# Differential attention's scores as three 64-row products per map instead of two 128-row ones

## The chip, the core and the metric

One core of a Trainium2 chip runs the whole program in one launch. The metric is the time on the device in microseconds; the kernel before takes 2785.16 us (median of three runs, 2784.28 to 2789.13).

## What is computed

Two encoder layers over 1024 tokens of width 1024. Layer 0 mixes tokens by neighbourhood attention, layer 1 by differential attention; each is followed by a gated convolutional feed-forward part and a gated embedding. The change concerns layer 1's mixer. It has 8 heads with two maps each, of width 64:

```python
s = jnp.einsum('bhmqd,bhmkd->bhmqk', qb, k).astype(jnp.float32) + bias[None, :, None]
a = jax.nn.softmax(s, axis=-1)
w = a[:, :, 0] - lam_full * a[:, :, 1]
return jnp.einsum('bhqk,bhkd->bhqd', w.astype(v.dtype), v)
```

For each head and each map m (0 or 1), scores of 1024 queries by 1024 keys come from products over 64 elements; a bias is added; the two softmaxes are subtracted with a weight lam and multiplied with the values.

## The kernel before

**Precision.** The kernel splits a float32 operand a into a high part (a rounded to float32r, a type whose products are one TensorE instruction each in this trace, where plain float32 ones are two) and a low part (a minus the high part), and forms a product as high x high + high x low + low x high: three matmuls, `mm3` (L104 to L109). `split` (L81) makes the parts: ScalarE writes the high part (L85), VectorE the low one (L86).

**Layer 1's mixer** (`da`, L578) works through 64 chunks; a chunk is one head h = n // 8 and one tile of 128 queries. What runs in a chunk, on TensorE strictly in the order of the program, since that engine alone is scheduled by hand (the other engines' lists are ordered by the framework's scheduler):

- `da_values` (L546) of the chunk before: 16 matmuls of 128 columns (two instructions for each of 8 plain float32 products, L553) into a bank of the pool `tr`.
- `da_scores` of the next chunk, map 0, then `da_turn(n, 0)`: four transposes (L539) of the finished weights E of this chunk into a bank of `tr`, copied to SBUF by ScalarE (L542).
- `tick(0.25)`, then `da_scores` of the next chunk, map 1, then `da_turn(n, 1)`: four more transposes, copied by VectorE (L544). In the text T0 and T1 are the transposes of the two turns.
- `tick(0.25)`, `da_out` of the chunk before (one transpose, L567, into the bank that `da_values` took), `tick(0.5)`.

`tick` moves a second stream of work forward, `qkv_stream` (L228), which projects the next heads' keys, queries and values: six steps per chunk, one step being one `mm3` with 512 columns (L107 to L109). So TensorE always has projections between the attention's own pieces.

**PSUM.** Pool `s` has two buffers of two banks (scores of 128 queries by 1024 keys), `pj` two banks for projections, `tr` two banks for transposes, values and outputs. A bank is given out again once its last reader is done; the values' bank is held from the first value matmul until `da_out` behind T1.

**Queries and keys.** A projected block has map 0 of a head on partitions 0 to 63 and map 1 on 64 to 127. So that a score matmul can use all 128 rows, the evacuation puts the parts on top of each other: for map m, `Q[m]` holds the high part on the map's own half and the low part on the other one, `KH[m]` holds the keys' high part on both halves and `KL[m]` the low part on both. With these, `Q[m]` by `KH[m]` and `Q[m]` by `KL[m]` (L515, L516) give all four products of parts in two matmuls. It costs, per block of 512 tokens and per map, ScalarE's high part (64 x 512, L249 and L267), VectorE's low part (L250, L268) and for keys two copies to the other half (on GpSimd in layer 0, L252 and L253; on VectorE in layer 1, L255 and L256). A head takes two pages A and B of pool `r2`, which has four.

**Softmax** (`softmax_pre`, L360): VectorE adds the bias to the scores and finds the row's extreme (L364), ScalarE exponentiates and sums (L368). With both maps done, VectorE forms the coefficient from the two sums (L525 to L527) and the difference of the two maps in place, E (L528).

Of the kernel before, what the change touches and what calls it, by code (L numbers as in the profile page):

```python
# [8 lines left out]
F32 = mybir.dt.float32  # L9
# [29 lines left out]
class Trunk:  # L39
# [188 lines left out]
    def qkv_stream(self, layer, hT, x, first, mid):  # L228
# [7 lines left out]
        for j in range(KT):  # L236
            A = self.page(self.r2, "r2", (P, 4, SEQ), F32R)
            B = self.page(self.r2, "r2", (P, 4, SEQ), F32R)
            Q, KH, KL = [A[:, 0], A[:, 1]], [A[:, 2], A[:, 3]], [B[:, 0], B[:, 1]]
            def keys(tb):  # L240
                s = slice(tb * 512, tb * 512 + 512)
                ps, a = begun.pop(0) if begun else (self.bank(self.pj), 0)
                for kt, _ in enumerate(self.proj(wk, hT, ps, tb, a)):
                    if tb == 0 and kt == (1, 6)[layer]:
                        values()
                    yield
                for m in range(2):
                    o, far = own[m], own[1 - m]
                    nc.scalar.activation(KH[m][o, s], ps[o], AF.Copy)  # L249
                    nc.vector.tensor_tensor(out=KL[m][o, s], in0=ps[o], in1=KH[m][o, s].bitcast(F32), op=ALU.subtract)  # L250
                    if layer == 0:
                        nc.gpsimd.tensor_copy(KH[m][far, s], KH[m][o, s].bitcast(F32))  # L252
                        nc.gpsimd.tensor_copy(KL[m][far, s], KL[m][o, s].bitcast(F32))  # L253
                    else:
                        nc.vector.tensor_copy(KH[m][far, s], KH[m][o, s].bitcast(F32))  # L255
                        nc.vector.tensor_copy(KL[m][far, s], KL[m][o, s].bitcast(F32))  # L256

            def queries(tb):
                s = slice(tb * 512, tb * 512 + 512)
                ps, a = begun.pop(0) if begun else (self.bank(self.pj), 0)  # L260
                for kt, _ in enumerate(self.proj(wq, hT, ps, tb, a)):
                    if j == 0 and tb == 0:
                        mid(kt)
                    yield
                for m in range(2):
                    o, far = own[m], own[1 - m]
                    nc.scalar.activation(Q[m][o, s], ps[o], AF.Copy, scale=-0.125)  # L267
                    nc.vector.scalar_tensor_tensor(  # L268
                        out=Q[m][far, s], in0=ps[o], scalar=-0.125, in1=Q[m][o, s].bitcast(F32),
                        op0=ALU.mult, op1=ALU.subtract,  # L270
                    )
# [12 lines left out]
            self.qk[j] = Q, KH, KL  # L284
# [218 lines left out]
    def da_scores(self, x, n, m):  # L503
        nc = self.nc
        mm = nc.tensor.matmul
        h, t = n // NT, n % NT
        Q, KH, KL = self.qk[h]
        if t == 0 and m == 0:
            self.T = self.page(x, "T", (P, TW))
            nc.sync.dma_start(self.T, self.skewed[h][:, P - 1 : P - 1 + TW])  # L510
        s = self.ps.tile([P, 1024], F32, tag="s", name=self.uid("s"))
        q = Q[m][:, t * P : t * P + P]
        for half in range(2):
            w = slice(half * 512, half * 512 + 512)
            mm(s[:, w], q, KH[m][:, w], start=True, stop=False)  # L515
            mm(s[:, w], q, KL[m][:, w], start=False, stop=True)  # L516
# [11 lines left out]
        nc.vector.scalar_tensor_tensor(out=w, in0=e, scalar=c, in1=w, op0=ALU.mult, op1=ALU.add)  # L528
# [49 lines left out]
    def da(self, hT, oT, first, mid):  # L578

        N = NT * D_HEADS  # L580
        with self.tc.tile_pool(name="xa1", bufs=2, reuse_waits="tile") as x, \
# [5 lines left out]
            self.da_scores(x, 0, 0)  # L587
            self.da_scores(x, 0, 1)
            self.tick(6 / 6)
            for n in range(N + 1):  # L590
# [9 lines left out]
                if n + 1 < N:  # L600
                    self.da_scores(x, n + 1, 1)
# [624 lines left out]
```

## Time and profile before

| what | value |
|---|---|
| runs | 2784.28, 2785.16, 2789.13 us |
| profiled execution's own time | 2788.92 us |
| its span | 2787.1 us |
| mean granted clock of TensorE | 0.987 |
| layer 1's attention, by first and last score work | about 1364 to 1946 us of the span |
| score matmuls of layer 1 (L515, L516) | 256 + 256, 512 columns each |
| value matmuls (L553) and transposes (L539) | 1024 and 512, 128 columns each |

The span is the time from the first to the last instruction that the profiler saw. A busy share counts time with at least one instruction in work; matmuls overlap their neighbours, so the distance between two starts, and not a duration, says how long one keeps TensorE. The profile lists TensorE's weight loads (PEld) apart from its matmuls (PE). A form such as `128*128 128x512` gives rows and columns of the array in use, then the operand's partitions and columns.

### The profile page before, as it was taken

The page shows a single profiled execution, that of the slowest core. Times are in us where ns is not written, and L with a number is a line of the kernel's source. Part 1 is how long each engine was busy: PE and PEld are TensorE (multiplying, and loading weights), DVE is VectorE, ACT ScalarE, POOL GpSimd, SP SyncE. Part 2 cuts the span into 40 slices and gives each one's busy share as a digit, 9 for nine tenths or more (in the row PEclk, how much of TensorE's full clock was granted, in tenths as well). Part 3 has the DMA queues.
Part 4 walks back from the last instruction along what each step waited for, and adds up shares of the span by engine and source line. Part 5 has one row for each costly group of instructions (what it writes and reads, how often), then busy time and mean ns, then how long its engine had stood idle before and what let it go on. Part 6 is the DMA issues. An engine that isn't in the chain of part 4 may idle for free.

```text
span 2787.1 us, 36499 instructions
## 1 busy us (share of the span) xinstructions
PE 2706.9 (97%) x13312; PEld 2260.9 (81%) x13312; DVE 1983.3 (71%) x3393; ACT 1341.0 (48%) x2477; POOL 495.0 (18%) x473
## 2 busy tenths in 40 slices
PE   7999999989999999999999999999989999999999
PEld 5788887868888888878888888887868888888877
DVE  5677776678777777666677777786687776777664
ACT  4555556444444435454455555566444444444442
POOL 2121220024433400001000000000023343300000
PEclk9999999999999999999999999999989999999999
DMA  6412214623332283343211111115413333372442
GB/s 187 164 52 67 64 49 157 156 81 106 106 110 91 106 283 107 102 147 106 98 45 45 45 45 45 38 43 177 136 68 106 108 105 106 112 270 92 118 141 99
DMA packets 129188, 298.48 MB, mean 107 GB/s; under 512 B 11720, under 2 KB 37704, under 8 KB 129008
## 3 DMA queue, kind: packets, MB, share of 16 engines
q1 hardware_dynamic: 129008, 296.15, 32.4%
q8 instruction: 104, 1.70, 0.3%
q14 instruction: 76, 0.62, 0.1%
HBM read 221.69 MB, written 86.61 MB: 111 GB/s over the span
## 4 chain that ended last, share of the span: by engine, by line
PE 89%; DMA 5%; DVE 3%; ACT 2%; issue 1%; SPq 0%; POOL 0%; ACTq 0%; DVEq 0%; POOLq 0%
PE b L107 21%; PE b L109 20%; PE b L108 20%; PE g L637 6%; PE m L637 5%; PE b L553 4%; PE s L515 2%; PE s L516 2%; PE b L539 2%; PE b L135 2%; PE av L426 2%; DVE r L86 1%; PE b L410 1%; DMA x<-in_x 1%; DMA raw<-in_qkv 1%; DMA raw<-in_ple_w_gate 1%
## 5 line engine op out<-in xcount | busy, mean ns | idle before, releaser
L107 PE MATMUL b<-r,ws 128*128 128x512 f32 (+1 forms) x1312 | 541.0, 412 | 3.2 <-ACT ws L85 3.2
L109 PE MATMUL b<-r,ws 128*128 128x512 f32 (+1 forms) x1312 | 512.9, 391 | 0.5 <-DVE ws L86 0.5
L108 PE MATMUL b<-r,ws 128*128 128x512 f32 (+1 forms) x1312 | 512.1, 390 | 0.6 <-DVE r L86 0.5
L107 PE MATMUL b<-r,wa 128*128 128x512 f32 x704 | 276.5, 393 | 28.1 <-ACT wa L85 27.2
L368 ACT ACTIVATE E<-E,mn 128x1024 f32<-128x1024 f32 (+2 forms) x256 | 221.6, 866 | 148.4 <-DVE mn L364 146.6
L109 PEld LDWEIGHTS b<-r,ws 128*128 128x128 f32 x1312 | 248.3, 189 | 53.3 <-DVE ws L86 1.0
L119 POOL TENSOR_TENSOR ss<-ss,mhalf 128x1 f32<-128x1 f32 x136 | 87.5, 644 | 1141.0 <-DVE ss L557 566.0
L107 PEld LDWEIGHTS b<-r,ws 128*128 128x128 f32 x1312 | 249.6, 190 | 48.8 <-ACT ws L85 3.6
L108 PEld LDWEIGHTS b<-r,ws 128*128 128x128 f32 x1312 | 250.0, 191 | 37.6 <-DVE r L86 1.9
L108 PE MATMUL b<-r,wa 128*128 128x512 f32 x704 | 275.8, 392 | 0.0
L109 PE MATMUL b<-r,wa 128*128 128x512 f32 x704 | 275.6, 391 | 0.0
L107 PE MATMUL b<-r,r 128*128 128x512 f32 x680 | 269.3, 396 | 5.0 <-DVE v L899 2.8
L108 PE MATMUL b<-r,r 128*128 128x512 f32 x680 | 265.4, 390 | 0.0
L109 PE MATMUL b<-r,r 128*128 128x512 f32 x680 | 265.3, 390 | 0.0
L86 DVE TENSOR_TENSOR r<-raw,r 128x512 fp32r<-128x512 f32 (+1 forms) x178 | 140.8, 795 | 111.8 <-ACT r L85 111.5
L85 ACT ACTIVATE r<-raw 128x512 fp32r<-128x512 f32 (+1 forms) x178 | 121.4, 687 | 205.2 <-PE b L108 166.2
L86 DVE TENSOR_TENSOR ws<-raw,ws 128x512 fp32r<-128x512 f32 (+3 forms) x168 | 155.3, 932 | 65.3 <-ACT ws L85 63.8
L85 ACT ACTIVATE ws<-raw 128x512 fp32r<-128x512 f32 (+3 forms) x168 | 124.3, 748 | 143.3 <-PE b L109 57.0
L637 PE MATMUL g<-r,ws 128*128 128x512 f32 x768 | 182.8, 398 | 8.5 <-DVE facc L1008 8.5
L364 DVE CUSTOM_DVE_ANT_0 E<-s,T 128x1024 f32<-128x1024 f32 x128 | 156.5, 1224 | 33.5 <-PE s L516 32.5
L107 PEld LDWEIGHTS b<-r,wa 128*128 128x128 f32 x704 | 133.3, 189 | 56.5 <-ACT wa L85 27.7
L637 PEld LDWEIGHTS g<-r,ws 128*128 128x128 f32 x768 | 146.4, 192 | 39.6 <-DVE facc L1008 9.4
(178 smaller groups left out, 5332.3 us busy)
## 6 DMA issues: line engine op xcount, KB each, us to landing
raw<-in_w_in SPq DMA_DIRECT2D x88, 512.0 KB, 3.5
raw<-in_qkv SPq DMA_DIRECT2D x48, 512.0 KB, 5.7
spillS<-r SPq DMA_DIRECT2D x88, 256.0 KB, 2.5
r<-in_ffn_w_out SPq DMA_DIRECT2D x40, 512.0 KB, 10.3
raw<-spillS SPq DMA_DIRECT2D x40, 512.0 KB, 3.5
spillA<-cv SPq DMA_DIRECT2D x66, 256.0 KB, 2.6
raw<-spillA SPq DMA_DIRECT2D x30, 512.0 KB, 3.8
x<-x SPq DMA_DIRECT2D x24, 512.0 KB, 3.7
```

The costliest lines, as they stand in the source:

```text
L85: nc.scalar.activation(hi, src, AF.Copy)
L86: nc.vector.tensor_tensor(out=lo, in0=src, in1=hi.bitcast(F32), op=ALU.subtract)
L107: mm(out, sta[0], mov[0], start=first, stop=False, skip_group_check=onto)
L108: mm(out, sta[0], mov[1], start=False, stop=False, skip_group_check=onto)
L109: mm(out, sta[1], mov[0], start=False, stop=last, skip_group_check=onto)
L119: self.nc.gpsimd.tensor_tensor(out=ss, in0=ss, in1=self.mhalf, op=ALU.pow)
L135: self.nc.tensor.transpose(t[:, k * P : k * P + P], h[:, c : c + P], self.ident)
L364: nc.vector.tensor_tensor_reduce(out=e, in0=s, in1=bias, scale=1.0, scalar=3e38, op0=ALU.add, op1=ALU.min, accum_out=mn)
L368: nc.scalar.activation(e, e, AF.Exp, bias=mn, scale=-1.0, accum_out=sm)
L426: nc.tensor.matmul(out, V[:, kb, m], a[:, at * P : (at + w) * P], start=i + z == 0, stop=i == len(steps) - 1 and z == 1)
L553: nc.tensor.matmul(o, wT[:, k], V[:, k], start=k == 0, stop=k == KT - 1)
L637: mm(out[half], a, b[:, w], start=first and k + z == 0, stop=last and k == n - 1 and z == 2)
```

## The change

In layer 1, queries and keys stay where the projection puts them: one page A per head holds queries' high and low parts and keys' high and low parts (A[:, 0] to A[:, 3]), each with map 0 on partitions 0 to 63 and map 1 on 64 to 127. `split` writes each with one ScalarE and one VectorE instruction over all 128 partitions; there are no copies to the other half. `da_scores` no longer takes m: it takes both score buffers and issues, for each half of the keys, three products for each map with 64 rows, map 0 and map 1 in turn. It drops the product of the two low parts. Both softmaxes follow, and both maps' scores now lie ahead of `da_turn(n, 0)`; nothing lies between the two turns but `tick(0.25)`. Layer 0 is as before.

```diff
         for j in range(KT):
             A = self.page(self.r2, "r2", (P, 4, SEQ), F32R)
-            B = self.page(self.r2, "r2", (P, 4, SEQ), F32R)
-            Q, KH, KL = [A[:, 0], A[:, 1]], [A[:, 2], A[:, 3]], [B[:, 0], B[:, 1]]
+            if layer == 0:
+                B = self.page(self.r2, "r2", (P, 4, SEQ), F32R)
+                Q, KH, KL = [A[:, 0], A[:, 1]], [A[:, 2], A[:, 3]], [B[:, 0], B[:, 1]]
...
+                if layer == 1:
+                    self.split(ps, A[:, 2, s], A[:, 3, s])
+                    return
                 for m in range(2):
                     o, far = own[m], own[1 - m]
                     nc.scalar.activation(KH[m][o, s], ps[o], AF.Copy)
                     nc.vector.tensor_tensor(out=KL[m][o, s], in0=ps[o], in1=KH[m][o, s].bitcast(F32), op=ALU.subtract)
-                    if layer == 0:
-                        nc.gpsimd.tensor_copy(KH[m][far, s], KH[m][o, s].bitcast(F32))
-                        nc.gpsimd.tensor_copy(KL[m][far, s], KL[m][o, s].bitcast(F32))
-                    else:
-                        nc.vector.tensor_copy(KH[m][far, s], KH[m][o, s].bitcast(F32))
-                        nc.vector.tensor_copy(KL[m][far, s], KL[m][o, s].bitcast(F32))
+                    nc.gpsimd.tensor_copy(KH[m][far, s], KH[m][o, s].bitcast(F32))
+                    nc.gpsimd.tensor_copy(KL[m][far, s], KL[m][o, s].bitcast(F32))
...
+                if layer == 1:
+                    self.split(ps, A[:, 0, s], A[:, 1, s], -0.125)
+                    return
...
-            self.qk[j] = Q, KH, KL
+            self.qk[j] = (Q, KH, KL) if layer == 0 else A
...
-    def da_scores(self, x, n, m):
+    def da_scores(self, x, n):
...
-        s = self.ps.tile([P, 1024], F32, tag="s", name=self.uid("s"))
-        q = Q[m][:, t * P : t * P + P]
+        s = [self.ps.tile([P, 1024], F32, tag="s", name=self.uid("s")) for _ in range(2)]
+        q = slice(t * P, t * P + P)
         for half in range(2):
             w = slice(half * 512, half * 512 + 512)
-            mm(s[:, w], q, KH[m][:, w], start=True, stop=False)
-            mm(s[:, w], q, KL[m][:, w], start=False, stop=True)
-        e = self.page(x, f"E{m}")
+            for z, (a, b) in enumerate(((0, 2), (0, 3), (1, 2))):
+                for m in range(2):
+                    o = slice(64 * m, 64 * m + 64)
+                    nc.tensor.matmul(s[m][:, w], A[o, a, q], A[o, b, w], start=z == 0, stop=z == 2)
         a = (NT - 1 - t) * P
-        sm = self.softmax_pre(s, self.T[:, a : a + SEQ], e)
-        if m == 0:
-            self.chunk[n] = e, sm
-            return
-        w, r0 = self.chunk[n]
+        e = [self.page(x, f"E{m}") for m in range(2)]
+        r0, sm = [self.softmax_pre(s[m], self.T[:, a : a + SEQ], e[m]) for m in range(2)]
+        w = e[0]
+        self.chunk[n] = w, r0
...
-            self.da_scores(x, 0, 0)
-            self.da_scores(x, 0, 1)
+            self.da_scores(x, 0)
...
-                    self.da_scores(x, n + 1, 0)
+                    self.da_scores(x, n + 1)
                 if n < N:
                     self.da_turn(x, n, 0)
                 self.tick(0.25)
-                if n + 1 < N:
-                    self.da_scores(x, n + 1, 1)
                 if n < N:
                     self.da_turn(x, n, 1)
```

More of the change, by code (lines that the diff above doesn't have):

```diff
@@ L527, in da_scores @@
         nc.vector.reciprocal(r0, r0)
-        nc.vector.scalar_tensor_tensor(out=w, in0=e, scalar=c, in1=w, op0=ALU.mult, op1=ALU.add)
+        nc.vector.scalar_tensor_tensor(out=w, in0=e[1], scalar=c, in1=w, op0=ALU.mult, op1=ALU.add)
     def da_turn(self, x, n, g):
```

5 lines of the change are left out of this document (2 added, 3 removed).

## The prediction

> **What bounds the kernel now.** I read the page's busy shares and its chain of waits first, then the table of stretches, then the groups by shape, and last the order of time inside one chunk of layer 1's attention.
>
> ```profile
> span 2787.1 us, 36499 instructions
> ...
> PE 2706.9 (97%) x13312; PEld 2260.9 (81%) x13312; DVE 1983.3 (71%) x3393; ACT 1341.0 (48%) x2477; POOL 495.0 (18%) x473
> ...
> PE 89%; DMA 5%; DVE 3%; ACT 2%; issue 1%; SPq 0%; POOL 0%; ACTq 0%; DVEq 0%; POOLq 0%
> ```
>
> TensorE is busy for 97% of the span and carries 89% of the chain. That average must hold in the stage that changes, which runs from 1364 to 1946 us. Two stretches of it, and one near its end (columns: us, then each engine's busy time and instructions, granted clock, DMA share, GB/s):
>
> ```profile
> 1420.00:1500.00 80.00, 79.94 (x468) 68.38 (x467) 62.02 (x122) 44.77 (x91) 5.10 (x9) 1.00 0.12 40
> ...
> 1740.00:1820.00 80.00, 79.93 (x467) 68.11 (x465) 62.46 (x124) 44.44 (x89) 5.02 (x9) 1.00 0.10 34
> ...
> 1880.00:1910.00 30.00, 29.32 (x174) 24.74 (x173) 23.14 (x40) 22.29 (x42) 1.64 (x3) 1.00 0.62 213
> ```
>
> TensorE has no hole (79.9 of 80 us) at full clock, VectorE is busy for 62 and ScalarE for 44. So only TensorE's own list counts here, and what the other engines lose or gain is worth something only where TensorE comes to wait for them. Only the last few chunks have small holes, beside the loads of the output weights.
>
> One chunk (of 64) in order of time:
>
> ```profile
> 1603.15 1.95 PE L553 MATMUL b<-v,wT 128*128 128x128 f32 x16
> ...
> 1604.68 1.27 DVE L528 SCALAR_TENSOR_TENSOR E<-E,c,E 128x1024 f32<-128x1024 f32 x1
> ...
> 1604.85 0.47 PE L515 MATMUL s<-r 128*128 128x512 f32 x1
> ...
> 1605.17 0.39 PE L516 MATMUL s<-r,r 128*128 128x512 f32 x1
> ...
> 1605.40 0.40 PE L515 MATMUL s<-r 128*128 128x512 f32 x1
> ...
> 1605.63 0.40 PE L516 MATMUL s<-r,r 128*128 128x512 f32 x1
> ...
> 1606.10 0.63 PE L539 MATMUL b<-ident,E 128*128 128x128 f32 x4
> ...
> 1606.48 0.47 PE L107 MATMUL b<-r,ws 128*128 128x512 f32 x1
> ...
> 1606.76 0.60 ACT L542 ACTIVATE wT<-b 128x512 f32<-128x512 f32 x1 [1.11 <-PE b L539]
> 1606.79 0.39 PE L108 MATMUL b<-r,ws 128*128 128x512 f32 x1
> ...
> 1607.02 0.39 PE L109 MATMUL b<-r,ws 128*128 128x512 f32 x1
> ...
> 1607.25 0.40 PE L515 MATMUL s<-r 128*128 128x512 f32 x1
> ...
> 1608.17 0.60 PE L539 MATMUL b<-ident,E 128*128 128x128 f32 x4
> ```
>
> Durations of neighbours overlap, so the price of a matmul is the distance of starts: a 512-column one holds TensorE for 0.23 us (1605.17, 1605.40, 1605.63), and I use 0.231. Sixteen 128-column ones take 1604.85 - 1603.15 = 1.70 us, 0.106 each, though 128 columns at the same rate would be 0.058: there the loading of weights sets the pace, at about 0.107 us a load. The order is: sixteen value matmuls, four score matmuls of map 0, four transposes T0 (L539), one stream step of three (L107 to L109), four score matmuls of map 1, four transposes T1, then more stream steps.
>
> **The change part by part.** I take one chunk at a time and multiply by 64.
>
> **(a) The products.** Eight 128-row matmuls (8 x 0.231 = 1.848 us) become twelve 64-row ones with the same 512 columns.
>
> ```profile
> L515 PE MATMUL s<-r 128*128 128x512 f32 x256 | 106.1, 414 | 0.0
> L516 PE MATMUL s<-r,r 128*128 128x512 f32 x256 | 100.5, 392 | 0.0
> ```
>
> These are 512 in all, 8 per chunk. The trace of before has no two matmuls on different rows side by side, so the price has two ends. Lower end: the halves of a pair run in the time of one, 6 x 0.231 = 1.386 us, a gain of 0.462; the twelve weight loads, 12 x 0.107 = 1.28 us, still fit beneath. Upper end: one after another, 12 x 0.231 = 2.772, a loss of 0.924. I take the lower end: two matmuls of a pair share no rows, no operands and no PSUM bank, and the only limit of the whole engine that a row shows beside the columns, the weight load, is below it. The second half may trail the first by one load (0 to 0.107 us, once per chunk at the end of the twelve); I take 0.05.
>
> The Trainium skill, "TensorE: Matmul & The Clock Gate", Part 3, says the same of matmuls in distinct row groups (starts some 4 ns apart); no run so far shows it. By that rule the trailing would be next to nothing and the sum 3 us lower.
>
> **(b) Going from whole rows to half rows and back.** Each chunk now goes over twice: behind the values, and ahead of T0. The nearest row is layer 0's table, the only matmuls with fewer rows (32*8), first TensorE and then its weight loads:
>
> ```profile
> 55.26 0.39 PE L109 MATMUL b<-r,ws 128*128 128x512 f32 x1
> 55.58 1.88 PE L491 MATMUL b<-r,t 32*8 32x512 f32 x4
> ```
> ```profile
> 55.04 0.19 PEld L109 LDWEIGHTS b<-r,ws 128*128 128x128 f32 x1
> 55.58 0.09 PEld L491 LDWEIGHTS b<-r,t 32*8 32x8 f32 x2 [0.35 <-issue]
> ```
>
> L109 has streamed its columns by 55.26 + 0.23 = 55.49, and the first load of the other shape starts only at 55.58, for no wait that the profile shows. So a change of shape may cost 0.09 us of emptying plus a load of 0.107 that is no longer hidden: 0.20 us, twice per chunk, less the 0.05 by which the load behind the values is bare already (0.107 - 0.058): 0.35 at most. Least: nothing, if that gap belongs to the table's plain float32 and not to its rows; a gain is excluded, since nothing is removed. I take 0.20, nearer to the row, which has the same kind of step but two differences.
>
> The Trainium skill, "TensorEngine Tiling (Array Packing)", Key Properties, speaks against this change: going from one tiling mode to another drains TensorE. The 0.09 us above agrees with it; by that rule the full 0.35 stands and the sum is 10 us higher, which is the second rival.
>
> **(c) The score products no longer lie between T0 and T1.** Both maps now come ahead of T0. The pool of transposes has two banks and one holds the values' product from its first matmul to L567 behind T1, so T0 and T1 share the other: T1 must wait for ScalarE's copy L542. That copy ends at 1606.76 + 0.60 = 1607.36, 1.26 us behind T0's start. Today 0.93 us of scores cover it (T1 at 1608.17). Without them T1 would come at 1607.25, where L515 stands: a wait of 0.11, and some 0.05 to hand over: 0.16 us per chunk. Behind T1 on TensorE stand stream steps and everything else, in order, so it is paid in full. Least nothing (a bank free by another way); most 0.75, if one half-row evacuation of 0.59 us (L249 below) stands ahead on ScalarE. I take 0.16, since ScalarE was idle ahead of the copy here (1.11).
>
> **(d) T0 gets more lead.** In the chunk shown T0 starts 0.47 us behind the last score matmul and not 0.23: it waited for E, ready at 1604.68 + 1.27 = 1605.95. With map 1's scores moved up, E(n) is done some 2 us sooner. All such waits together:
>
> ```profile
> PEld b L539 <- PE s L516: 3.3, 7, 0.5
> ...
> PEld b L539 <- ACT wT L542: 0.9, 2, 0.8
> ```
>
> The L516 named had long ended, so these are E's: I take 3 us in all as won. The second row shows that the copy of (c) does hold back transposes.
>
> **(e) Splitting queries and keys.**
>
> ```profile
> L268 DVE SCALAR_TENSOR_TENSOR r<-b,r 64x512 fp32r<-64x512 f32 x64 | 44.1, 689 | 5.7 <-ACT r L267 4.0
> L250 DVE TENSOR_TENSOR r<-b,r 64x512 fp32r<-64x512 f32 x64 | 44.0, 687 | 16.0 <-ACT r L249 14.9
> L249 ACT ACTIVATE r<-b 64x512 fp32r<-64x512 f32 x64 | 37.7, 589 | 18.3 <-PE b L109 11.7 <-DVE r L250 5.2
> L86 DVE TENSOR_TENSOR r<-b,r 128x512 fp32r<-128x512 f32 x48 | 32.3, 688 | 5.4 <-ACT r L85 4.9
> L256 DVE CAST r<-r 64x512 fp32r<-64x512 f32 x32 | 13.5, 422 | 0.9
> L255 DVE CAST r<-r 64x512 fp32r<-64x512 f32 x32 | 13.5, 422 | 1.0
> ```
>
> Half of L249, L250 and L268 is layer 1's. VectorE drops 32 of 0.687, 32 of 0.689 and 64 copies of 0.422, and gains 32 of 0.688 (L86's row at full height): 71 - 22 = 49 us less; ScalarE drops about 18. All of it lies beside the 79.9 of 80 us of TensorE: nothing. If that cover were gone, up to 49 us would show, but no wait in the stretches above says so. The single page per head leaves two more pages of the pool free, so the embedding's loads and splits near the end can start sooner; TensorE did not wait for them, and I give that nothing either. Four weight loads and matmuls more per chunk are in (a).
>
> **The sum.** Per chunk -0.462 + 0.05 + 0.20 + 0.16 = -0.052 us; by 64 it is -3.3, with (d) -6.3 us. The profiled execution took 2788.9 us (span 2787.1 and 1.8 around it), so 2782.6 of its own; it lies 3.8 above the median of the runs, 2785.2, from which the same sum gives 2779.
>
> **The rivals.**
>
> *The halves run one after another.* One mechanism: TensorE gives each 64-row matmul its own 0.231 us. For it: every row of the trace shows one 512-column matmul at a time, at the same pace. Against: none has disjoint rows. Price: +0.924 + 0.20 + 0.16 = 1.28 us per chunk, +82, with (d) 79: 2864 (2841 with neither switch nor wait). It decides from a pair time of about 0.24 us upward, where the gain of (a) no longer pays for (b) and (c).
>
> *They overlap, but the switches eat it.* Full 0.35, full trailing 0.107 and 0.16: +0.155 per chunk, +10, with (d) +7: 2792; to 2815 if ScalarE is late for the copy in some chunks. For it: the gap at 55.49. Against: its different data type.
>
> *They overlap only in part.* If each half's load waits until that half's own matmul has streamed, a pair takes 0.231 + 0.107 = 0.338: 2.03 for six, +0.18 + 0.20 + 0.16 = 0.54, +35, with (d) +31: 2816. Against it stand today's loads, which start with the matmul ahead of them and not at its end:
>
> ```profile
> 1600.27 0.39 PE L107 MATMUL b<-r,ws 128*128 128x512 f32 x1
> 1600.27 0.19 PEld L108 LDWEIGHTS b<-r,ws 128*128 128x128 f32 x1
> ```
>
> *They overlap and nothing eats it.* No switch and no trailing: -0.462 + 0.16 = -0.302, -19, with (d) -22: 2763; without the T1 wait 2753.
>
> **How the numbers follow.** Forecast (2769 to 2790, likeliest 2779) 0.42; one after another 0.20; switches eat it 0.14; in part 0.08; nothing eats it 0.16. A difference of 0.2%, 5.6 us, is about what a measurement here can tell from no change, so "same" is 2779.6 to 2790.8. Of the forecast's 0.42 about 0.22 lies below that and 0.20 inside; with 0.16 that makes faster 0.38. Of the second rival 0.03 lies inside: same 0.23. The rest, 0.11 + 0.08 + 0.20, is slower: 0.39. The range leaves out the lowest part of the last rival and the upper half of the first: 2762 to 2862. The forecast's own range is 2769 to 2790.
>
> **What would show it.** In the changed profile: the two matmuls of a pair starting well under 0.23 us apart and pairs 0.23 to 0.25 apart (a); a gap ahead of the first 64-row weight load and behind the last (b); T1's loads waiting for L542's successor, about 0.15 us a chunk, 10 us in all (c); no wait of T0 for E (d); VectorE near 55 of 80 us (62 less 49 / 64 for each of nine chunks) in the same stretches, TensorE still full but for (c) (e). Twelve starts 0.23 us apart would make the prediction wrong by the first rival; a chunk shorter by over 0.2 us, by the last.

## The result, and the profile after

The changed kernel takes **2802.82 us** (median of four runs, 2799.62 to 2806.07) where the kernel before, on the same chip, takes 2787.14. The ratio is **1.0057, interval 1.0044 to 1.0070**: slower by some 16 us. The forecast was 2779, faster by 6; the range held the time, the direction was wrong. The execution profiled after took 2799.62 us, its span is 2797.8.

The page of the changed kernel, span and busy shares:

```profile
span 2797.8 us, 36876 instructions
...
PE 2709.0 (97%) x13568; PEld 2231.2 (80%) x13568; DVE 1929.5 (69%) x3297; ACT 1317.4 (47%) x2445; POOL 493.9 (18%) x473
```

TensorE has 256 more instructions and is busy for 2 us more, while the span grew by 11: most of the rest is time in which it stands still. Where it does is told by the starts of the value matmuls of chunks 10, 54 and 61. In the kernel before:

```profile
1469.46 0.27 PE L553 MATMUL b<-v,wT 128*128 128x128 f32 x1
...
1861.32 0.27 PE L553 MATMUL b<-v,wT 128*128 128x128 f32 x1
...
1926.05 0.27 PE L553 MATMUL b<-v,wT 128*128 128x128 f32 x1
```

In the changed one:

```profile
1464.02 0.27 PE L557 MATMUL b<-v,wT 128*128 128x128 f32 x1
...
1859.30 0.27 PE L557 MATMUL b<-v,wT 128*128 128x128 f32 x1
...
1938.12 0.27 PE L557 MATMUL b<-v,wT 128*128 128x128 f32 x1
```

Over 44 chunks the mean goes from 391.86 / 44 = 8.906 to 395.28 / 44 = 8.984 us, 3.4 us in all. Over the seven chunks behind them it goes from 64.73 to 78.82 us: **14.1 us in seven chunks**, chunks 55 to 61, called the tail below. Two losses, then: a small one in every chunk, and a large one in the tail.

**The steady chunk.** One chunk of the changed kernel in order of time, TensorE:

```profile
1607.92 1.95 PE L557 MATMUL b<-v,wT 128*128 128x128 f32 x16
1609.80 1.67 PE L522 MATMUL s<-r 64*128 64x512 f32 x12
1611.40 0.66 PE L543 MATMUL b<-ident,E 128*128 128x128 f32 x4
1611.81 0.47 PE L107 MATMUL b<-r,ws 128*128 128x512 f32 x1
1612.12 0.39 PE L108 MATMUL b<-r,ws 128*128 128x512 f32 x1
1612.35 0.40 PE L109 MATMUL b<-r,ws 128*128 128x512 f32 x1
1612.74 0.44 PE L543 MATMUL b<-ident,E 128*128 128x128 f32 x2
```

Twelve 64-row matmuls take 1.60 us to the next piece; six at 0.231 would be 1.386, so they do run in pairs. Windows of some 20 ns around the moments at which a new pair starts show it (a row of x4 holds the new pair and the one still in work, and gives the start of the older):

```profile
1609.80 0.50 PE L522 MATMUL s<-r 64*128 64x512 f32 x2
...
1609.80 0.74 PE L522 MATMUL s<-r 64*128 64x512 f32 x4
1610.14 0.64 PE L522 MATMUL s<-r 64*128 64x512 f32 x4
1610.37 0.64 PE L522 MATMUL s<-r 64*128 64x512 f32 x4
1610.60 0.64 PE L522 MATMUL s<-r 64*128 64x512 f32 x4
```

The pairs start at 1609.80, 1610.14, 1610.37 and 1610.60, 0.23 us apart behind the first. Now the edges. The sixteen value matmuls take 1609.80 - 1607.92 = 1.88 us to the first score, against 1.70 before: 0.18 going in. Of the 1.60 above, 0.21 is more than six pairs; some 0.10 of that is the first matmul behind the values, which before has too (1604.85 to 1605.17 and not 0.23): 0.11 coming out, and the four transposes take 0.41 and not 0.38. **Both switches together: 0.32 us in these two chunks**, and 0.36 by the medians of 44 chunks, where the transposes before take 0.35 (in the chunk shown they had waited for E). The weight loads show the second switch and the wait of T1:

```profile
1611.40 0.42 PEld L543 LDWEIGHTS b<-ident,E 128*128 128x128 f32 x4 [0.36 <-issue]
...
1612.74 0.31 PEld L543 LDWEIGHTS b<-ident,E 128*128 128x128 f32 x3 [0.43 <-ACT wT L546]
```

T1 starts 0.39 us behind L109 where the next matmul would start 0.23 behind: a wait of 0.16. All of them together, in the waits of 1380 to 1850 us:

```profile
PEld b L543 <- ACT wT L546: 22.2, 52, 0.4
...
PEld b L543 <- issue: 18.9, 52, 0.4
```

Both come 52 times, once in each chunk of the stretch; in a part of each 0.4 us the matmul ahead is still in work. VectorE and ScalarE have lost work (62.02 and 44.77 before), and TensorE is still full:

```profile
1420.00:1500.00 80.00, 80.00 (x498) 63.79 (x498) 52.71 (x107) 40.71 (x84) 4.95 (x9) 1.00 0.14 48
```

**The tail.** Busy time and granted clock of chunks 55 to 61 (the clock stands behind the five engines, ahead of the last two numbers), first before, then after with two short stretches inside it:

```profile
1861.32:1926.05 64.73, 61.86 (x360) 51.84 (x358) 50.57 (x92) 48.59 (x91) 3.83 (x7) 1.00 0.50 169
```

```profile
1859.30:1938.12 78.82, 66.45 (x387) 51.42 (x386) 51.30 (x92) 48.83 (x91) 3.85 (x7) 0.96 0.41 139
...
1871.30:1874.70 3.40, 3.32 (x15) 3.32 (x16) 1.56 (x3) 1.00 (x3) 0.00 (x0) 0.50 0.07 19
1912.00:1915.40 3.40, 3.40 (x11) 2.54 (x10) 3.33 (x7) 3.18 (x7) 0.00 (x0) 0.54 0.40 112
```

TensorE stands idle for 78.82 - 66.45 = 12.4 us where it stood for 2.9: +9.5. And its clock is granted at 0.96 on average, at half in two stretches of 3.4 us: 0.04 x 78.82 = 3.2 us more. With seven steady chunks' 0.12 each, 0.8, these make 13.5 of the 14.1. Its waits in the seven chunks:

```profile
PE b L107 <- ACT ws L1101: 3.5, 3, 1.7
PE b L557 <- ACT ot L579: 3.3, 1, 3.3
PE b L543 <- ACT wT L546: 2.5, 2, 2.2
PE b L638 <- ACT ws L1101: 1.8, 1, 1.8
```

These are the four longest in total, and in every one TensorE waits for a copy or an evacuation on ScalarE, which is busy for 48.8 of 78.8 us only. ScalarE's list, around the two longest:

```profile
1868.88 1.06 ACT L85 ACTIVATE r<-raw 128x1024 fp32r<-128x1024 f32 x1 [2.08 <-DMA raw<-in_ple_w_proj]
...
1870.98 0.35 ACT L579 ACTIVATE ot<-b,subg 128x128 f32<-128x128 f32 x1
...
1909.69 1.06 ACT L85 ACTIVATE r<-raw 128x1024 fp32r<-128x1024 f32 x1 [2.39 <-DMA raw<-in_da_w_o]
1910.65 0.58 ACT L546 ACTIVATE wT<-b 128x512 f32<-128x512 f32 x1
```

and on TensorE:

```profile
1871.38 3.65 PE L557 MATMUL b<-v,wT 128*128 128x128 f32 x16 [3.29 <-ACT ot L579]
...
1911.28 0.66 PE L543 MATMUL b<-ident,E 128*128 128x128 f32 x4 [2.18 <-ACT wT L546]
```

ScalarE waits for a weight block that hasn't landed, to split it (L85); the copy behind it in its list waits too (in the first case with an exponential between the two), and with it TensorE. Behind the first stop the sixteen value matmuls take 3.6 us to the next piece and not 1.9: that is the clock's half rate.

Why are the blocks late? The first two blocks of the output weights leave late, because the SP queue issues them behind stores that wait for ScalarE in turn:

```profile
1871.35 11.48 SPq L580 DMA_DIRECT2D oT<-ot  x2
...
1883.84 1.21 SPq L96 DMA_DIRECT2D raw<-in_da_w_o  x2
```

The two blocks of the waits above have another reason. The pool `raw` into which blocks are loaded has three buffers (L53), and a load leaves when VectorE's part of an earlier split (L86) has freed one. For the second:

```profile
1904.00 1.22 DVE L86 TENSOR_TENSOR r<-raw,r 128x1024 fp32r<-128x1024 f32 x1
...
1905.25 3.32 SPq L96 DMA_DIRECT2D raw<-in_da_w_o  x2
```

This load leaves at 1905.25, 0.03 us behind the end of that L86, and the split that needs it starts 4.44 us later. The first (in_ple_w_proj) leaves at 1864.04, just as close behind another L86, and its split starts 4.84 us later. From the third on, all six blocks of the output weights leave in this way. So splits wait for loads, and loads wait for splits.

### The profile page after: what moved, and what is told of

Its sections match the earlier page's. It is cut to its first block, busy times and chain, and to the rows that moved or that the text cites. A ratio compares the mean times of both kernels' runs of the same rounds, so it can differ in the third digit from the quotient of the medians.

```text
span 2797.8 us, 36876 instructions
## 1 busy us (share of the span) xinstructions
PE 2709.0 (97%) x13568; PEld 2231.2 (80%) x13568; DVE 1929.5 (69%) x3297; ACT 1317.4 (47%) x2445; POOL 493.9 (18%) x473
## 4 chain that ended last, share of the span: by engine, by line
PE 87%; DMA 6%; DVE 4%; ACT 2%; issue 1%; POOL 0%; SPq 0%; ACTq 0%; POOLq 0%; DVEq 0%
PE b L107 20%; PE b L109 20%; PE b L108 20%; PE g L638 6%; PE m L638 5%; PE b L557 4%; PE s L522 3%; PE b L543 3%; PE b L135 2%; DVE r L86 2%; PE av L430 2%; PE b L414 1%; DMA x<-in_x 1%; DMA raw<-in_qkv 1%; DMA raw<-in_ple_w_gate 1%
## 5 line engine op out<-in xcount | busy, mean ns | idle before, releaser
L109 PE MATMUL b<-r,ws 128*128 128x512 f32 (+1 forms) x1312 | 512.9, 391 | 0.5 <-DVE ws L86 0.5
L109 PEld LDWEIGHTS b<-r,ws 128*128 128x128 f32 x1312 | 248.2, 189 | 53.3 <-DVE ws L86 1.0
L109 PE MATMUL b<-r,wa 128*128 128x512 f32 x704 | 275.6, 391 | 0.0
L109 PE MATMUL b<-r,r 128*128 128x512 f32 x680 | 265.8, 391 | 0.0
L86 DVE TENSOR_TENSOR r<-raw,r 128x512 fp32r<-128x512 f32 (+1 forms) x178 | 140.6, 795 | 119.8 <-ACT r L85 119.5
L85 ACT ACTIVATE r<-raw 128x512 fp32r<-128x512 f32 (+1 forms) x178 | 121.4, 689 | 202.1 <-PE b L108 158.6
L86 DVE TENSOR_TENSOR ws<-raw,ws 128x512 fp32r<-128x512 f32 (+3 forms) x168 | 154.8, 929 | 68.3 <-ACT ws L85 65.1
L85 ACT ACTIVATE ws<-raw 128x512 fp32r<-128x512 f32 (+3 forms) x168 | 124.4, 749 | 144.1 <-PE b L109 56.9
L107 PEld LDWEIGHTS b<-r,r 128*128 128x128 f32 x680 | 128.1, 188 | 36.4 <-ACT ws L1101 4.8
```

The lines of the kernel that those rows point to most:

```text
L85: nc.scalar.activation(hi, src, AF.Copy)
L86: nc.vector.tensor_tensor(out=lo, in0=src, in1=hi.bitcast(F32), op=ALU.subtract)
L107: mm(out, sta[0], mov[0], start=first, stop=False, skip_group_check=onto)
L109: mm(out, sta[1], mov[0], start=False, stop=last, skip_group_check=onto)
```

## The experiments

Below, "steady" is the median distance of two chunks' value matmuls in the middle of the attention (8.77 before, 8.89 in the changed kernel), "tail" the time of the seven chunks 55 to 61 (64.7 and 78.8). Every ratio is against the kernel before, run beside it.

### Do the halves overlap, and does the order of issue matter?

*The products of one map behind those of the other*, six to a half of the keys:

```diff
-            for z, (a, b) in enumerate(((0, 2), (0, 3), (1, 2))):
-                for m in range(2):
+            for m in range(2):
+                for z, (a, b) in enumerate(((0, 2), (0, 3), (1, 2))):
```

> The changed kernel, with the three products of map 0 issued ahead of the three of map 1 in each half of the keys, instead of in turn. Nothing is left out. Theory (neighbours on different halves of the rows share the array's time): of twelve 64-row matmuls only those where one map follows the other overlap, three places per chunk, so nine slots of 0.231 us and not six: +0.69 us per chunk, +44 us over the changed kernel, about 2847 us; starts within a map 0.23 us apart, at a change of map near 0. Rival (it is the smaller height of the matmuls, not who stands beside them): time as the changed kernel, 2803. If nothing overlapped at all: twelve slots, +89, 2892.

Measured: 2800.61 us, ratio 1.0047 (1.0035 to 1.0060), steady 8.89. The theory missed: nothing got slower. The time is the rival's, but the run after this one shows that the rival's reason, the smaller height, isn't it either. The same windows of 20 ns:

```profile
1613.66 0.50 PE L522 MATMUL s<-r 64*128 64x512 f32 x2
...
1614.00 0.63 PE L522 MATMUL s<-r 64*128 64x512 f32 x4
```

The pairs start together as before, though in the program three matmuls of map 0 come first. So TensorE doesn't keep these two halves in step with the program: each works through its own matmuls. (The rows don't say to which map a matmul belongs; that a pair is made of one of each follows from the next run, where two on the same rows don't overlap.)

*Both maps on the same 64 rows:*

```diff
-                    o = slice(64 * m, 64 * m + 64)
+                    o = slice(0, 64)
```

> The changed kernel with all twelve score matmuls of a chunk on partitions 0 to 63: map 1's scores are left out and computed as map 0's again, with the same number and shape of instructions. Theory (two 64-row matmuls share the array's time only on different halves): twelve slots of 0.231 us in place of six, +1.39 us per chunk, +89, about 2892. Rival (a 64-row matmul is just cheaper): 2803.

Measured: 2879.48 us, ratio 1.0334 (1.0319 to 1.0348), steady 10.22, +1.33 against the expected 1.39.

```profile
1618.80 3.01 PE L522 MATMUL s<-r 64*128 64x512 f32 x12
1621.74 0.66 PE L543 MATMUL b<-ident,E 128*128 128x128 f32 x4
```

Twelve take 2.94 us here and 1.60 in the changed kernel. What makes the overlap is that the two stand on different rows, and the first rival's price, 0.231 us for each, was right for matmuls on the same rows.

### The price of a switch

*The scores in two pieces, one ahead of each turn*, so that a chunk goes over to half rows twice:

```diff
-    def da_scores(self, x, n):
+    def da_scores(self, x, n, half):
...
                 self.tick(0.25)
+                if n + 1 < N:
+                    self.da_scores(x, n + 1, 1)
```

> The changed kernel with the second half of the keys' score matmuls moved behind T0 and its stream step: six 64-row matmuls, T0, three stream matmuls, six 64-row matmuls, T1. So TensorE goes from whole to half rows and back twice per chunk instead of once. Nothing is left out. Theory (a way there costs about 0.19 us and a way back 0.16, wherever they lie): +0.35 us for the second pair of switches, -0.22 us since the scores again cover T0's copy: +0.13 to +0.18 us per chunk, +8 to +12 over the changed kernel's 2803, about 2812. Rival (the gaps around the scores come from their neighbours, values and transposes, and not from the switch): only the copy's wait goes, 2789.

Measured: 2814.71 us, ratio 1.0105 (1.0089 to 1.0120), steady 9.07.

```profile
1613.19 0.40 PE L109 MATMUL b<-r,ws 128*128 128x512 f32 x1
1613.52 0.96 PE L523 MATMUL s<-r 64*128 64x512 f32 x6
1614.41 0.66 PE L546 MATMUL b<-ident,E 128*128 128x128 f32 x4
1614.83 0.47 PE L107 MATMUL b<-r,ws 128*128 128x512 f32 x1
```

L109 to the first score takes 0.33 and not 0.231, three pairs 0.89 and not 0.693, the transposes 0.42 and not 0.38: 0.34 us for the second pair of switches. The chunk grew by 0.18 only, since T1's wait is covered again; that is worth 0.21 by the next run, which would leave 0.13, and 0.05 is not accounted for.

### The wait of T1

*Three stream steps between the turns rather than one:*

```diff
                 if n < N:
                     self.da_turn(x, n, 0)
-                self.tick(0.25)
+                self.tick(0.5)
                 if n < N:
                     self.da_turn(x, n, 1)
-                self.tick(0.25)
```

> The changed kernel with three stream steps between the two transposing turns and none between the second turn and the output (before: one and two). Nothing is left out. Theory (T1 waits for ScalarE's copy out of the bank that T0 used, 0.22 us a chunk by the profile after): the wait goes, steady chunks take 8.65 instead of 8.88 us, -14 us: 2789. If the late copies near the end of the stage are what costs there, some of those 13 us go too: down to 2780. Rival (the gap ahead of T1 has another cause, such as a drain of TensorE): 2803, gap unchanged.

Measured: 2787.11 us, ratio 1.0000 (0.9992 to 1.0009), steady 8.68. In the waits of 1380 to 1850 us the switch is left and the wait for L546 is gone:

```profile
PEld b L543 <- issue: 19.7, 54, 0.4
```

So T1's wait cost 8.89 - 8.68 = 0.21 us a chunk. Against before the chunk is 0.09 us shorter: with 0.44 won by the products that leaves 0.35 for the switches. At chunk 54 this kernel is 8.6 us ahead of the one before (1.8 of it from ahead of the attention), and at the end it is level: its tail takes 73.8.

*The kernel before with both maps ahead of T0*, whole rows, one step between the turns:

```diff
                     self.da_scores(x, n + 1, 0)
+                    self.da_scores(x, n + 1, 1)
...
                 self.tick(0.25)
-                if n + 1 < N:
-                    self.da_scores(x, n + 1, 1)
```

> The kernel before (128-row products, two pages, copies to the other half) with both maps' scores ahead of the first turn, as the change has it. Nothing is left out. Theory (the new order alone costs 0.22 us a chunk for T1 and gives back T0's waits, some 3 us): steady chunks 8.95 us instead of 8.75, +11 us: 2798, and no gap around the scores. Loss in the last ten chunks: if it comes from T1 standing close behind T0, it shows here too (another +13, 2811); if it comes from the half-height products or the single page, it does not. Rival (order costs nothing, the half-height products all): 2787.

Measured: 2855.89 us, ratio 1.0248 (1.0234 to 1.0262), steady 10.09. It missed by 58 us. ScalarE's list in one chunk:

```profile
1609.32 1.15 ACT L368 ACTIVATE E<-E,mn 128x1024 f32<-128x1024 f32 x1 [1.73 <-DVE mn L364]
...
1610.47 0.58 ACT L542 ACTIVATE wT<-b 128x512 f32<-128x512 f32 x1
```

T0's matmuls lie between 1608.71 and 1609.06, but the copy stands behind map 0's exponential. L109 of the one step starts at 1609.61, so T1 could start at 1609.84; it starts 1.26 us later:

```profile
1611.10 0.66 PE L539 MATMUL b<-ident,E 128*128 128x128 f32 x4 [1.09 <-ACT wT L542]
```

The same move that costs 0.21 beside 64-row products costs 1.3 here, by where one exponential stands in another engine's list.

*The same with three steps between the turns:*

```diff
-                self.tick(0.25)
-                if n + 1 < N:
-                    self.da_scores(x, n + 1, 1)
+                self.tick(0.5)
```

> The kernel before (128-row products, two pages, copies to the other half) with both maps' scores ahead of the first turn and three stream steps between the turns. Nothing is left out. For the steady chunks: T0's copy, which in the run with whole rows and the maps first ended 2.35 us behind T0, is covered by 2.46 us, so 8.72 us a chunk, 3 us won over the kernel before. For the last ten chunks, theory A (they lose because both maps' softmaxes come at once and ScalarE's list is ordered anew around them): +9 to +11 there, 2792. Theory B (the loss there comes with the half-height products or the single page): none, 2783.

Measured: 2787.75 us, ratio 1.0009 (1.0000 to 1.0018), steady 8.83 and not the 8.72 expected, tail 66.7. With whole rows and both maps together the tail is nearly that of before: the order of the maps is not what loses it.

### What loses the tail

*Queries and keys on two pages again:*

```diff
-            if layer == 0:
-                B = self.page(self.r2, "r2", (P, 4, SEQ), F32R)
+            B = self.page(self.r2, "r2", (P, 4, SEQ), F32R)
...
-                    self.split(ps, A[:, 2, s], A[:, 3, s])
+                    self.split(ps, B[:, 0, s], B[:, 1, s])
```

> The changed kernel with the keys' parts on a second page per head, so that a head takes two pages of the pool as before the change; same instructions otherwise. Nothing is left out. Theory A (the last ten chunks lose 13 us because the freed pages let the embedding's loads and splits change places with the attention's work on ScalarE): the end is as before, 2790. Theory B (pages do not matter; the last chunks lose because T1 and the values stand behind ScalarE's splits that wait for loads, in an order that comes from the half-height products): 2803. Steady chunks 8.88 us in both.

Measured: 2804.61 us, ratio 1.0061 (1.0047 to 1.0074), tail 79.1. The page that came free has nothing to do with it.

*Half of the output weight's eight blocks loaded early*, into that page; with three steps between the turns, and without:

```diff
+            if layer == 1 and j == KT - 2:
+                self.early = self.page(self.r2, "r2", (P, 4, D))
+                for k in range(4):
+                    nc.sync.dma_start(self.early[:, k], self.i["da_w_o"][k * P : k * P + P])
```

> The changed kernel with three stream steps between the turns (as in the run with the steps between) and with four of the eight row blocks of the output weights loaded two heads sooner into the page that the change freed; only their splits stay at the end. Nothing is left out. Theory (the last ten chunks lose because ScalarE's splits wait for these loads with T0's copy, the embedding's evacuations and the outputs queued behind them): of the 9 us lost there against the kernel before most go, 2779. Rival (the loss is not the loads but the amount or order of work on ScalarE there): 2787 as without the early load.

> The changed kernel as it is, with the same early load of four row blocks of the output weights alone. Nothing is left out. Theory (loads): 13 us at the end of the stage become some 4, 2793; steady chunks unchanged at 8.88 us. Rival (ScalarE's work or its order): 2803.

Measured: 2791.58 us, ratio 1.0024 (1.0015 to 1.0033), and 2804.03, ratio 1.0066 (1.0053 to 1.0079). The theory missed in both; the second has the rival's time. In the first, ScalarE makes four splits in a row from 1855.60 on, 3.9 us, and the values wait 4.7 us for its copy of ot. Against the run with the steps alone, chunks 57 to 61 take 5.5 us less and chunks 55 and 56 take 7.1 us more: the loss moved, and did not shrink.

*The splits on GpSimd instead of ScalarE and VectorE*: the output weight's, with steps between; the embedding's as well; both in the kernel before; every second block; the four early blocks.

```diff
+        if aside:
+            for s in (slice(0, 512), slice(512, D)):
+                self.nc.gpsimd.tensor_copy(hi[:, s], raw[:, s])
+                self.nc.gpsimd.tensor_tensor(out=lo[:, s], in0=raw[:, s], in1=hi[:, s].bitcast(F32), op=ALU.subtract)
+            return hi, lo
```

> The changed kernel with three stream steps between the turns and with the eight row blocks of layer 1's output weights split by GpSimd (in halves of 512 columns, both parts) instead of ScalarE and VectorE. Nothing is left out. Theory (the last ten chunks lose where a split of these blocks, still waiting for its load, stands in ScalarE's list ahead of the attention's copies): of the 9 us lost there against the kernel before, the waits at the four late chunks go, some 6 us: 2781. The wait of the values for the output's copy at chunk 55 stays, since that is the embedding's split. Rival (the loss moves to GpSimd's square roots behind the splits, or to the loads themselves, which now free their buffers later): 2787 or above.

> As the run with the output weights' splits on GpSimd, and the four splits of layer 1's embedding inputs there as well. Nothing is left out. Theory (splits that wait for loads in ScalarE's list): the wait at chunk 55 goes too, 9 us or more in all against 2787, 2778 or less, below the kernel before. Rival (GpSimd, at some 4.5 us a block, is late with the last blocks and the first output products wait): 2785 or above.

> The kernel before with the same twelve splits on GpSimd and nothing else changed. Nothing is left out. Theory: the kernel before has some 5 us of such waits in its last ten chunks (chunks 56, 58, 59 and 61 are 0.5 to 1.4 us above 8.77), so 2782. If it gains as much as the changed kernel with the steps does, the half-row products are worth no more than the steps' 0.07 us a chunk, 4 us, over whole rows.

> The changed kernel with three stream steps between the turns and with every other row block of layer 1's output weights (four of eight) split by GpSimd, the rest by ScalarE and VectorE. Nothing is left out. Theory (the last ten chunks lose at splits in ScalarE's list; GpSimd alone was 10 us late with all eight): chunks 57 to 60 keep most of the gain of the run with all eight aside (8.7 us each) and the 9.9 us wait at chunk 61 goes: 2780. Rival (four splits that wait for loads are enough to hold the copies up): 2787.

> As that, but the four blocks that GpSimd splits are the first four, loaded two heads sooner into the page that the change freed. Nothing is left out. Theory: GpSimd starts as soon as the operands of the projections are free, no load is waited for, and the other four loads come while it works: chunks 55 to 61 take within 5 us in all of 8.68 each, 2779. Rival (the loads that ScalarE's list still waits for cost the same): 2787.

Measured:

| splits on GpSimd | us | ratio | tail |
|---|---|---|---|
| output weights | 2787.67 | 1.0009 (1.0000 to 1.0018) | 74.4 |
| and the embedding's | 2794.32 | 1.0028 (1.0018 to 1.0038) | 79.9 |
| both, kernel before | 2804.33 | 1.0066 (1.0053 to 1.0079) | 85.0 |
| every second block | 2788.50 | 1.0007 (0.9998 to 1.0015) | 74.3 |
| the four early blocks | 2789.33 | 1.0012 (1.0003 to 1.0022) | 77.5 |

In the first, chunks 57 to 60 run at 8.66 to 8.68 us: with the splits off ScalarE's list nothing is lost there. But GpSimd takes 1.4 us on the mean for 128x512 of the low part, and TensorE stands for 9.6 us at the first product with the output weights. It waits there for ScalarE's split of the attention's outputs, whose load leaves only at 1921.02, when GpSimd's part of a split has freed a buffer of `raw` (1920.99). In the second and third it waits 10.0 and 8.7 us at the same place. With every second block aside, the splits left on ScalarE wait 9.0 us for their loads. With the early blocks aside, TensorE waits 4.7 us for a normalisation that starts at 1871.68: its root, behind GpSimd's splits, had come at 1865.75, and VectorE's list had a copy and a chunk's difference of the two maps ahead of it.

*The stores that wait for ScalarE off the SP queue*; with steps, in the kernel before, and in the changed kernel alone:

```diff
-            nc.sync.dma_start(oT[h][:, cols], ot)
+            nc.scalar.dma_start(oT[h][:, cols], ot)
...
-            nc.sync.dma_start(self.pp[layer][s], e)
+            (nc.scalar if layer == 1 else nc.sync).dma_start(self.pp[layer][s], e)
```

> The changed kernel with steps between the turns (as the run that did so before, 2787 us), and with the stores of ot and the second layer's stores of ws issued from ScalarE's queue right behind what makes them, so that the loads of the output weight on the SP queue no longer stand behind them. Theory Q (the loss of the last ten chunks is late loads, whose splits stand in ScalarE's list ahead of the copies that TensorE waits for): the loads leave the SP queue over 15 us earlier, chunks 55 to 61 run within 0.4 us of the steady 8.68 but for one, and the time is 2779 us (2776 to 2782). Rival R (it is ScalarE's own work in its order, not the loads' lateness): 2787 us as before, the splits no longer waiting but the copies as late.

> The kernel before with the same stores issued from ScalarE's queue. Theory Q: its own chunks 55 to 61 lose 3 to 8 us over the steady chunk, so 2781 us (2778 to 2784). Rival R: 2786 us, no difference.

> The changed kernel with the same stores issued from ScalarE's queue, no steps between the turns. Theory Q: the 13 us of the last ten chunks shrink to 3 or less, so 2792 us (2788 to 2796). Rival R: 2803 us, as the changed kernel.

Measured: **2783.83 us, ratio 0.9987 (0.9978 to 0.9996)**; 2786.33, 1.0000 (0.9990 to 1.0009); 2804.51, 1.0059 (1.0046 to 1.0071). The first loads do leave earlier, in the first of these runs from 1865.41 on instead of 1879.85:

```profile
1865.41 37.37 SPq L96 DMA_DIRECT2D raw<-in_da_w_o  x7
```

but the tails are 70.1, 65.5 and 78.5 us. Only the first fell (from 73.8), and its stretch says by what:

```profile
1854.96:1925.03 70.07, 61.91 (x388) 49.60 (x386) 50.19 (x90) 48.63 (x91) 3.83 (x7) 1.00 0.47 156
```

TensorE stands idle for 8.2 us, against 8.6 without the edit; what is gone is the half clock (1.00 here, 0.96 there). These are single executions, but the granted clock of all eleven runs of each says the same: 0.9896 on the mean against 0.9884, some 3 us of the span (the kernel before, run beside them: 0.9885 and 0.9881).

Theory Q's times missed. Yet the edit moved only the first two of the eight loads. The third leaves at 1889.33 (1888.90 without the edit), again behind an L86, and in the changed kernel with the stores moved ScalarE's splits wait for these loads as long as in the changed kernel itself (5.6 us in the tail there):

```profile
ACT r L85 <- DMA raw<-in_da_w_o: 5.5, 3, 2.4
```

So the stores are not what makes the tail, but the lateness of the other six loads was not taken away, and what it costs stays open.

*That kernel with every second split on GpSimd too:*

```diff
+                            aside=aside and kt % 2 == 0)
```

> The run with steps between the turns and the stores on ScalarE's queue (2784 us), with every second one of the eight splits of the output weight made by GpSimd too. That run's chunks 55 to 61 still stand 9.3 us over seven steady ones, where the kernel before has 2.7. Theory S (what is left of the loss is ScalarE's own work on the splits, 4 of 8 of which leave it): the 9.3 us halve or better, and the time is 2779 us (2776 to 2781). Rival G (GpSimd is late with its splits or with the roots, as in the runs with splits aside before): a chunk waits for GpSimd, and the time is 2784 us or more.

Measured: 2782.85 us, ratio 0.9984 (0.9975 to 0.9993), tail 69.7. Half the splits off ScalarE changed nothing beyond the interval; theory S fell. This and the run before it are the two fastest here, both faster than the kernel before by less than 0.2%.

**What stays open** is why TensorE stands idle in the tail for 8 to 13 us with half rows that overlap and splits on ScalarE, and for 3 with whole rows (4.5 with both maps first and three steps between; 10.9 with one step, of which seven times the copy's wait of 1.09 are 7.6). Shown: in the changed kernel the waits are for ScalarE's copies and evacuations, the longest behind splits in its list that wait for loads; with all eight splits of the output weights off that list, chunks 57 to 60 lose nothing. Shown too: neither the page, nor the stores, nor half of the splits is the cause alone, and four blocks loaded early move the loss. In the runs with the stores on ScalarE's queue and steps between, 2.2 to 2.6 us of the waits are for VectorE's normalisation.

Two rivals are left. One is the order of ScalarE's list. In the run with both maps on the same rows, every engine's instructions stand in exactly the order that they have in the changed kernel, so the scheduler that ordered the lists did not tell the two cases apart; and there, where the halves run one after another, TensorE's idle time in the tail is 79.6 - 72.8 = 6.8 us, not 12.4, with the clock at 1.00. In both, the eight splits of the output weights stand 0 to 1 chunk earlier in ScalarE's list than before, 0.4 on the mean (counted by the exponentials ahead of them). That would fit lists made for slower scores than the chip's. Against it stand the runs with three steps between the turns: there all eight but one stand where they do before, and TensorE is still idle for 8.2 to 8.6 us. The other rival is the pool `raw`: with few buffers, each late split makes a later load late. Neither the order on ScalarE nor the number of buffers was changed in any run.

## Why the prediction was wrong

**(a) The products: right.** Pairs 0.23 us apart, the halves 3 to 26 ns; trailing some 0.02 where I took 0.05. Both rivals about serial or partial overlap are out.

**(b) The switches: mis-sized.** The row of layer 0's table was the right one, and its gap plus a bare load gave 0.35. I took 0.20, "nearer to the row", but kept a discount for the table's other data type that no row supported. Measured 0.32 to 0.36, and 0.34 by the run that adds a second pair: with 0.35, +0.15 x 64 = 9.6 us over the sum. By the drain rule that I had weighed against it (the Trainium skill, "TensorEngine Tiling (Array Packing)", Key Properties) the full 0.35 stood; the measured 0.32 to 0.36 agree.

**(c) T1's wait: right.** The gap is the 0.16 us forecast (0.39 - 0.23); the whole cost, by the run with three steps, is 0.21 a chunk, +3.2 us over the sum. That it stayed so small is in part luck: I had put at most a half-row evacuation ahead of the copy, 0.75 in all, and in the run with whole rows the same wait is 1.26, because an exponential stands there.

**(d) right.** Between 1380 and 1850 us no wait of T0 for E is left. Its worth is an estimate: over 44 chunks the mean lay (8.906 - 8.767) x 44 = 6.1 us above the median chunk before and lies (8.984 - 8.889) x 44 = 4.2 above it now, which makes 2 us, 3 in all 64.

**(e) right in the steady part and wrong in the tail.** VectorE's work fell by 53.8 us in the whole program (1983.3 to 1929.5) where I said 49, and all of it is hidden in the steady part. But I said of the embedding's loads and splits near the end that "TensorE did not wait for them, and I give that nothing". They, and the output weight's, are what ScalarE has ahead of the copies TensorE waits for: **+13 us that no term of the sum held**. This is the step that failed: the tail got nothing for a reason that held in the kernel before alone. That the waits are these is shown; why half rows make them longer is not. The stretch of 1880 to 1910 us that I quoted already showed TensorE at 29.3 of 30, no longer full; I took a stage with holes for one like the others. A quarter of the tail's new loss, 3.2 of 9.5 + 3.2 us, is not even waiting but the clock that waiting takes away. The second rival came closest: its 2792 is the steady part, and "to 2815 if ScalarE is late for the copy in some chunks" is the tail, with a chance of 0.14 and no cause named.

By terms: -6.3 + 9.6 + 3.2 - 1.9 (trailing) + 13.3 = +18 us, and from chunk 0 to chunk 63 the profile grew from 561.1 to 579.0 us. (The span grew by 11 only, because chunk 0 comes 6 us sooner in this execution than in the one of before.) The runs grew by 15.7. Without (b) and the tail the forecast direction would have stood.

## What to carry to other kernels

A change of the rows in use cost TensorE about 0.35 us there and back here, so half-row products pay only where many of them stand together. Taking work out from between two steps that share a buffer exposes the other engine's copy; put something else there (here, two steps of a second stream were worth 0.21 us a chunk). And a stage with small holes before is a stage of its own: price it apart, since there the place of a copy in an engine's list, and not that engine's busy time, can decide.

## What the runs showed that I had not expected

- **The two halves don't follow the program's order between them.** Three matmuls of map 0 ahead of three of map 1 run as fast as in turn: steady 8.89 in both, pairs together at 1613.66 and 1614.00. Had each matmul to start behind the one ahead of it in the program, map 1's first could not start before map 0's third, and a chunk would be some 0.69 us longer (three slots of 0.231). The Trainium skill, "TensorE: Matmul & The Clock Gate", Part 3, says that matmuls start and end in program order; the measurement says otherwise for halves on different rows.
- **Short stops can cost clock.** Behind the stops of 3.29 and 2.18 us shown above, TensorE's clock was granted at 0.50 and 0.54 for 3.4 us, and sixteen value matmuls took 3.6 us instead of 1.9; in the run with three steps between the turns a stop of 1.93 us was enough. Two stops of 1.7 and 1.8 in the changed kernel's tail, and one of 2.7 us in the run with the stores moved and steps between, cost none. The Trainium skill, "TensorE: Matmul & The Clock Gate", Part 1, has half rate behind an idle window of some 3.4 us whose phase runs freely. The half rate, its length and the chance in it agree; stops well short of 3.4 us were enough here.
